# Pair products of a two-layer trunk: matmuls ordered by width, left operands prepared by parallel tasks, rotary tables begun earlier

## The chip, the cores and the metric

The kernel runs on one core of a Trainium2 chip, as one launch. The metric is the device time of one execution in microseconds; the time before is the median of three runs. All weights come from device memory in each execution.

## The reference

Two decoder layers over 512 positions, model width 1024, in float32. Each layer is a half-weighted gated feed-forward (FFN), a mixer (block-sparse attention in layer 0, a state-space mixer in layer 1), and another FFN. Cut to what the change touches, which are the four FFNs and the rotary tables of the attention:

```python
def swiglu(x, w_gate, w_up, w_down):
    return (jax.nn.silu(x @ w_gate) * (x @ w_up)) @ w_down

for i in range(2):
    x = x + 0.5 * swiglu(rms_norm(x, ffn1_norm[i]), ffn1_w_gate[i], ffn1_w_up[i], ffn1_w_down[i])
    h = rms_norm(x, mix_norm[i])
    x = x + moba_mixer(h, ...) if i == 0 else x + mamba2_mixer(h, ...)
    x = x + 0.5 * swiglu(rms_norm(x, ffn2_norm[i]), ffn2_w_gate[i], ffn2_w_up[i], ffn2_w_down[i])

# moba_mixer: q and k are turned by cos and sin of positions * inv_freq (rope)
```

The hidden width of an FFN is 2816, that is 22 tiles of 128.

## The kernel before

**Precision.** A float32 operand is split into a high part (rounded to the matmul's fp32r format) and a low part (the rest). A plain product then takes three matmuls: high by high, high by low, low by high. For weights, ScalarE (ACT) writes the high part (`whi`) from the loaded tile `wraw`, and VectorE (DVE) writes the low part (`wlo`). The task `halve_weights` does this piece by piece, 1024 columns at most, into a ring of four `whi` and four `wlo` buffers. Loads go out from SyncE's queue; a few sums of two weight tiles are made by accumulating transfers from GpSimd's (POOL's) queue.

**An FFN.** The hidden tiles stand in groups 0 to 5, 6 to 9, 10 to 13, 14 to 17 and 18 to 21 (`GROUPS`). Group 0 is computed plainly (`plain`). Each later group has two pairs of tiles (`pair`), and between their products stand the down projections of the group before (`down`). An FFN has eight pairs, so the four FFNs have 32 pairs.

**A pair.** For two hidden tiles, the 1024 inputs are cut in two halves and the 512 positions in two halves of 256, and a scheme of seven block products in place of eight is used. `PAIR` gives their order: A11, A12, A21-A22, -S2, A12-S2, a down projection, A11-A21, a down projection, A22, two down projections. The names are the left operands, blocks of the normed activations and their sums. Each left operand lies in four tiles `side` (k = 0 to 3) of 512 columns: 256 of the high part and 256 of the low part. One product (`product`) is, for two output halves o and four k, one matmul of 512 columns with `whi` (high weights by both parts) and one of 256 columns with `wlo` (low weights by the high part): 16 matmuls, alternating 512, 256, 512, 256. There are 32 x 7 = 224 products.

Products write three accumulators of two PSUM banks each: `x_`, `z_` and `y_`. Between products they are read: after A11 a task `read` copies half of `x_` (ACT) and adds the other half (DVE) into a tile; call it c1. After A12, `c11` makes two DVE additions from `z_`, and a gate follows (`ga`, ACT then DVE). After A21-A22 another `read` makes c5 from `y_`, again an ACT copy and a DVE addition. A12-S2 accumulates into `y_` and so may begin only when c5 has been read; the code waits for it with `yield When(lambda: "c5" in box)`. All those tiles are named `c` in the profile.

**Left operands.** The task `spread` (rank 60) makes the 28 `side` tiles of an FFN: for each k it scales two activation tiles into `xa` and `xb` (DVE), then one after the other, in place, the sums and differences (DVE, 256 columns), and for each left operand an ACT copy to the high part and a DVE subtraction for the low part (`sided`). One k is finished before the next begins.

**Order.** The order of instructions on every engine is written when the program is built, by a planner: tasks ask for tiles and instructions, and the planner issues the one that it thinks can start first, ties going to the lower rank. TensorE's main task has the rank `MAIN`; halving has `EASY` plus its due time, or `URGENT`. The chip then runs each engine's list in order, waiting on semaphores. The rotary tables (`rope_tables`: 14 small DVE operations, two sines on ACT, 18 POOL operations) are spawned by `midway`, at the first pair of group 3 of the first FFN, at rank `EASY - 1`, just ahead of the halving.

Most instructions are issued by one helper line (L221), so the profile is read by tile names.

Of the kernel before, what the change touches and what calls it, by code (L numbers as in the profile page):

```python
# [21 lines left out]
OP = mybir.AluOpType  # L22
# [18 lines left out]
GROUPS = ((0, 6), (6, 10), (10, 14), (14, 18), (18, 22))  # L41
# [10 lines left out]
MAIN, EASY, URGENT = 1e6, 1e5, -1.0  # L52
# [95 lines left out]
class Scheduler:  # L148
# [14 lines left out]
    def spawn(self, gen, prio=None):  # L163
        self.count += 1
        self.tasks.append(Task(gen, 100 + 0.01 * self.count if prio is None else prio))
        self.step(self.tasks[-1], None)
# [169 lines left out]
def trunk(ctx, tc, xT, pos, consts, cols, rows, wgu, wd, wqk, wv, wo, win, wz, wdt, wout, outT):  # L336
    nc = tc.nc
    V, S, PE, GP, SP = (Instructions(e, n) for e, n in (("DVE", nc.vector), ("ACT", nc.scalar), ("PE", nc.tensor), ("POOL", nc.gpsimd), ("SP", nc.sync)))
# [54 lines left out]
    def job(src, step=2.73, total=None, whole=False, term=None, name=None):  # L393


        n = src.shape[-1]
        if name:
            sources[name] = len(jobs)
        if term is not None:
            terms[len(jobs)] = sources[term] if isinstance(term, str) else term  # L400
        jobs.append((src, n, step, whole))
        needed.append(needed[-1] + (step * n / 512 if total is None else total))
# [24 lines left out]
    def down_job(i, what):  # L427
        job(down_src(i, what[2], what[1]))
# [5 lines left out]
    def pair_jobs(i, pair, downs):  # L434

        (b11, b21), (b12, b22) = ((wgu[i, j, :, :1024], wgu[i, j, :, 1024:]) for j in pair)
        right = {"A11": (b11, None), "A12": (b21, None), "A21-A22": (b12, b11), "-S2": (b22, "A21-A22"),
                 "A12-S2": (b22, None), "A11-A21": (b12, b22), "A22": (b21, "-S2")}
        downs = iter(downs)
        for nm in PAIR:  # L440
            if nm is None:
                down_job(i, next(downs))
            else:
                src, term = right[nm]
                job(src, step=2.78, total=2.78, whole=True, term=term, name=nm)

    for l in range(2):
        for i in (2 * l, 2 * l + 1):
# [140 lines left out]
    class Norm:  # L589
# [30 lines left out]
        def spread(self):  # L620


            yield When(lambda: self.rb is not None)
            for k in range(4):
                xa, xb = yield [slot("xa"), slot("xb")]
                for t, kk in ((xa, k), (xb, k + 4)):
                    op = V.scalar_tensor_tensor(t, x[kk], self.gain[:, kk:kk + 1], self.rb, op0=OP.mult, op1=OP.mult)
                    yield op.frees(*([self.rb] if kk == 7 and not self.plain else []))
                self.spread_left -= 2
                a11, a21, a12, a22 = xa[:, :256], xa[:, 256:], xb[:, :256], xb[:, 256:]  # L630
                yield from self.sided("A11", k, a11)
                yield from self.sided("A12", k, a12)
                yield from self.sided("A22", k, a22)
                yield V.tensor_tensor(a22, a21, a22, op=OP.subtract)
                yield from self.sided("A21-A22", k, a22)
                yield V.tensor_tensor(a22, a22, a11, op=OP.subtract)
                yield from self.sided("-S2", k, a22)
                yield V.tensor_tensor(a12, a12, a22, op=OP.add)
                yield from self.sided("A12-S2", k, a12, xb)
                yield V.tensor_tensor(a11, a11, a21, op=OP.subtract)  # L640
                yield from self.sided("A11-A21", k, a11, xa)

        def sided(self, nm, k, src, *done):
            t = yield slot("side", FR)
# [51 lines left out]
    def ffn(i, nrm, done, midway=None):  # L696
# [21 lines left out]
        def plain(j, last):  # L718
            p = take(wgu[i, j])
            pg, pu = yield [bank("pg"), bank("pu")]  # L720
            for u in range(2):
                for o, ps in ((0, pg), (1, pu)):
                    yield unit(p, 2 * u + o)
                    un = units[p][2 * u + o]
                    for kk in range(4):
                        k = 4 * u + kk
                        yield When(lambda: nrm.h[k] is not None)
                        ops = mm3(ps, cut(un, 128 * kk, 128 * kk + 128), nrm.h[k], k == 0, k == KT - 1)
                        if kk == 3:
                            ops[-1].frees(*un)  # L730
                        if last and o == 1:
                            ops[-1].frees(*nrm.h[k])
                        yield ops
            spawn(gated(pg, pu, j))

        def pair(j0, j1, downs, last):

# [2 lines left out]

            p = used[0]
            used[0] += 7 + len(downs)
            place = dict(zip(PAIR, range(p, p + len(PAIR))))
            out = {}

            def product(nm, ps, first):
                p = place[nm]
                Q.done_us = needed[p]
                yield unit(p, 0)
                un = units[p][0]  # L750
                for o in range(2):
                    for k in range(4):
                        yield When(lambda: nrm.left[nm][k] is not None)
                        a = nrm.left[nm][k]
                        b, c = 512 * o + 128 * k, 512 * o
                        ops = [PE.matmul(ps[:, c:c + 512], un[0][:, b:b + 128], a, start=first and k == 0, stop=False,
                                         skip_group_check=True),
                               PE.matmul(ps[:, c:c + 256], un[1][:, b:b + 128], a[:, :256], start=False, stop=k == 3,
                                         skip_group_check=True)]
                        if o and k == 3:  # L760
                            ops[-1].frees(*un)
                        if last and o:
                            ops[-1].frees(a)
                        yield ops

            def parts(ps):
                v = ps.rearrange("p (o h c) -> p o h c", o=2, h=2)
# [56 lines left out]
                yield from gate(j0, 1, t)  # L824

            x_, z_, y_ = None, None, None
            downs = iter(downs)
            seat = p
            for nm in PAIR:
                if nm is None:  # L830
                    assert used[0] > seat
                    keep, used[0] = used[0], seat
                    yield from down(*next(downs)[1:])
                    used[0] = keep
                elif nm == "A11":
                    x_ = yield bank("px", 2)
                    yield from product(nm, x_, True)
                    spawn(read(x_, "c1", box), 6)
                elif nm == "A12":
                    z_ = yield bank("pz", 2)  # L840
                    yield from product(nm, z_, True)
                    spawn(c11(z_), 6)
                elif nm == "A21-A22":
                    y_ = yield bank("py", 2)
                    yield from product(nm, y_, True)
                    spawn(read(y_, "c5", box), 6)
                elif nm == "-S2":
                    yield When(lambda: "c1" in box)
                    yield from product(nm, x_, False)
                    spawn(read(x_, "c2", box), 6)  # L850
                elif nm == "A12-S2":
                    yield When(lambda: "c5" in box)
                    yield from product(nm, y_, False)
                    spawn(c12(y_), 6)
                elif nm == "A11-A21":
                    yield When(lambda: "c2" in box)
                    yield from product(nm, x_, False)
                    spawn(c22(x_), 6)
                else:
                    yield When(lambda: "read" in box)  # L860
                    yield from product(nm, x_, False)
                    spawn(c21(x_), 6)
                seat += 1

        def down(g, n):
            p = take(down_src(i, n, g))
# [15 lines left out]
        for what in ffn_order(i):  # L882
            if isinstance(what, int):
                yield from plain(what, what == GROUPS[0][1] - 1)
            elif what[0] == "down":
                yield from down(*what[1:])
            else:
                if midway and what[0][0] == GROUPS[3][0]:
                    midway()
                yield from pair(*what[0], what[1], what[0] == (NH - 2, NH - 1))  # L890

# [477 lines left out]
    norms = [Norm(g) for g in gains]  # L1369

    def main():
        yield from ffn(0, norms[0], norms[1].add, lambda: spawn(rope_tables(), EASY - 1))
        yield from attention(norms[1], norms[2].add)
        yield from ffn(1, norms[2], norms[3].add)
        yield from ffn(2, norms[3], norms[4].add)
        yield from mamba(norms[4], norms[5].add)
        yield from ffn(3, norms[5], write)
# [94 lines left out]
```

## Time and profile before

| what | value |
|---|---|
| median of 3 runs | 2076.02 us (2075.43 to 2077.53) |
| profiled execution: its own time, its span | 2074.4 us, 2072.6 us |
| TensorE (PE) busy, share of the span | 2055.7 us, 99% |
| VectorE, ScalarE, GpSimd busy | 1490.8, 1034.4, 446.9 us |
| TensorE clock granted, mean of the span | 0.999 |
| matmul records: pair products, all | 3584, 10212 |

A busy PE is not a PE at its peak: matmuls overlap in the array, each record lasts longer than the distance to the next one, and the durations add up to more than the span. So the cost of a matmul is read as the distance from its start to the next start, and a wait shows as a distance that is longer than its neighbours'.

### The profile page before, as it was taken

How to read it: one execution, taken by the hardware profiler on the slowest of the kernel's cores; microseconds unless marked ns; L12 is line 12 of the kernel's file. 1: busy time of each engine (PE TensorE's matmuls, PEld its weight loads, DVE VectorE, ACT ScalarE, POOL GpSimd, SP SyncE). 2: the span in 40 equal slices, each digit the busy share in tenths (PEclk: the TensorE clock that was granted, in tenths of full speed). 3: DMA queues.
4: the chain of work that ended last, by engine and by line, in shares of the span. 5: the costliest groups of instructions: out<-in, count | busy, mean ns of one | idle time of the engine just before them, and what ended most of it. 6: DMA issues, size and time to landing. Idle time of an engine off the chain costs nothing.

```text
span 2072.6 us, 27874 instructions
## 1 busy us (share of the span) xinstructions
PE 2055.7 (99%) x10212; PEld 1721.8 (83%) x10212; DVE 1490.8 (72%) x2259; ACT 1034.4 (50%) x1756; POOL 446.9 (22%) x441
## 2 busy tenths in 40 slices
PE   9999999999999999999999999999999999999999
PEld 7788888888878888888888887888888888888887
DVE  6867877668879667778767776667575877767775
ACT  5544445454544444445444445674747645444442
POOL 1201211333231111102101011244343543101110
PEclk9999999999999999999999999999999999999999
DMA  7678895321135879854678884333332333678882
GB/s 251 159 190 213 207 229 154 102 67 66 62 107 129 203 200 225 216 164 117 179 190 213 219 212 150 91 94 112 91 103 92 102 112 110 153 194 210 218 217 77
DMA packets 102665, 321.31 MB, mean 155 GB/s; under 512 B 11520, under 2 KB 12160, under 8 KB 102528
## 3 DMA queue, kind: packets, MB, share of 16 engines
q1 hardware_dynamic: 84096, 252.42, 38.7%
q0 software_dynamic: 18432, 67.12, 18.5%
q8 instruction: 80, 1.31, 0.3%
q14 instruction: 57, 0.47, 0.1%
HBM read 283.77 MB, written 2.16 MB: 138 GB/s over the span
## 4 chain that ended last, share of the span: by engine, by line
PE 94%; DVE 3%; ACT 1%; POOL 1%; DMA 1%; issue 1%; SPq 0%; DVEq 0%; ACTq 0%; POOLq 0%
PE banks L221 94%; DVE wlo L221 1%; POOL ropea L221 0%; ACT whi L221 0%; DMA x<-xT 0%; DMA wraw<-wgu 0%; DVE c L221 0%; DVE xb L221 0%; DVE side L221 0%; SPq L221 0%; DVE xlo L221 0%; DVE ropeb L221 0%; POOL rstd L221 0%; ACT sq L221 0%; DVE rs_a L221 0%
## 5 line engine op out<-in xcount | busy, mean ns | idle before, releaser
L221 ACT ACTIVATE whi<-wraw 128x1024 fp32r<-128x1024 f32 (+1 forms) x531 | 498.2, 939 | 630.0 <-issue 303.2
L221 DVE TENSOR_TENSOR wlo<-wraw,whi 128x1024 fp32r<-128x1024 f32 (+1 forms) x531 | 589.2, 1111 | 188.0 <-ACT whi L221 187.3
L221 PE MATMUL banks<-side,whi 128*128 128x512 f32 x1792 | 639.3, 399 | 6.8 <-DVE c L221 4.0
L221 PE MATMUL banks<-side,wlo 128*128 128x256 f32 x1792 | 503.4, 281 | 0.7 <-DVE wlo L221 0.7
L221 PEld LDWEIGHTS banks<-side,whi 128*128 128x128 f32 x1792 | 336.7, 188 | 96.1 <-DVE c L221 14.5
L221 PEld LDWEIGHTS banks<-side,wlo 128*128 128x128 f32 x1792 | 338.7, 189 | 4.9 <-DVE wlo L221 1.2
L221 PE MATMUL banks<-hhi,whi 128*128 128x512 f32 x704 | 276.8, 393 | 0.0
L221 PE MATMUL banks<-hhi,wlo 128*128 128x512 f32 x704 | 275.5, 391 | 0.0
L221 PE MATMUL banks<-hlo,whi 128*128 128x512 f32 x704 | 274.7, 390 | 0.0
L221 PE MATMUL banks<-xhi,whi 128*128 128x512 f32 x648 | 259.1, 400 | 1.3 <-ACT xhi L221 1.3
L221 PE MATMUL banks<-xlo,whi 128*128 128x512 f32 x648 | 253.6, 391 | 1.4 <-DVE xlo L221 1.4
L221 PE MATMUL banks<-xhi,wlo 128*128 128x512 f32 x648 | 253.4, 391 | 0.0
L221 DVE TENSOR_TENSOR c<-banks,c 128x512 f32<-128x512 f32 x256 | 175.8, 687 | 45.3 <-PE banks L221 35.8
L221 PEld LDWEIGHTS banks<-hhi,wlo 128*128 128x128 f32 x704 | 132.2, 188 | 30.0
L221 PEld LDWEIGHTS banks<-hhi,whi 128*128 128x128 f32 x704 | 132.2, 188 | 28.8
L221 POOL DMA_DIRECT2D wraw<-wgu x64 | 56.5, 882 | 450.6 <-DMA wraw<-wgu 191.5
L221 DVE SCALAR_TENSOR_TENSOR x<-banks,x 128x512 f32<-128x512 f32 x160 | 110.4, 690 | 59.7 <-PE banks L221 58.6
L221 PEld LDWEIGHTS banks<-hlo,whi 128*128 128x128 f32 x704 | 132.4, 188 | 25.0
L221 POOL DMA_DIRECT2D wraw<-wraw x64 | 56.9, 888 | 441.8 <-DMA wraw<-wgu 210.7
L221 PEld LDWEIGHTS banks<-xlo,whi 128*128 128x128 f32 x648 | 121.6, 188 | 27.8 <-DVE xlo L221 2.6
L221 PEld LDWEIGHTS banks<-xhi,whi 128*128 128x128 f32 x648 | 121.5, 187 | 27.0 <-ACT xhi L221 1.6
L221 PEld LDWEIGHTS banks<-xhi,wlo 128*128 128x128 f32 x648 | 121.4, 187 | 26.4
(201 smaller groups left out, 2905.6 us busy)
## 6 DMA issues: line engine op xcount, KB each, us to landing
wraw<-wgu SPq DMA_DIRECT2D x270, 512.0 KB, 4.7
wraw<-wgu POOLq DMA_DIRECT2D x64, 512.0 KB, 8.2
wraw<-wraw POOLq DMA_DIRECT2D x64, 512.0 KB, 5.9
wraw<-wd SPq DMA_DIRECT2D x128, 256.0 KB, 4.1
wraw<-win SPq DMA_DIRECT2D x32, 512.0 KB, 3.8
wraw<-wd SPq DMA_DIRECT2D x32, 384.0 KB, 3.9
wraw<-wqk SPq DMA_DIRECT2D x16, 512.0 KB, 4.0
wraw<-wz SPq DMA_DIRECT2D x16, 512.0 KB, 3.8
```

Source lines behind the costliest of these rows:

```text
L221: op.fn(*op.args, **op.kw)
```

## The change

In `product` the two matmuls of a step are no longer issued together: all eight of 512 columns with `whi` come first, then all eight of 256 columns with `wlo`. In `spread` the one chain becomes four kinds of tasks with ranks of their own (60 to 66, by the order in which the products use the operands), with two more tiles per k (`xd`, `xe`) in place of sums made in place. `gated`, the gate of the plain tiles, gets rank 50. The rotary tables are spawned at the first pair of group 2 (hidden tiles 10 and 11) and not of group 3, two pairs sooner, at rank 2 x `EASY`, behind the halving. `pair_order` gives the order that `PAIR` gave, since every pair has four down projections.

```diff
+    def pair_order(downs):
+        rest = iter(downs)
+        order = [next(rest, None) if nm is None else nm for nm in PAIR]
+        return [nm for nm in order if nm is not None] + list(rest)
...
                 xa, xb = yield [slot("xa"), slot("xb")]
+                Q.uses[xa.tensor.name] = Q.uses[xb.tensor.name] = 4
...
-                a11, a21, a12, a22 = xa[:, :256], xa[:, 256:], xb[:, :256], xb[:, 256:]
-                yield from self.sided("A11", k, a11)
-                yield from self.sided("A12", k, a12)
-                yield from self.sided("A22", k, a22)
-                yield V.tensor_tensor(a22, a21, a22, op=OP.subtract)
-                yield from self.sided("A21-A22", k, a22)
-                yield V.tensor_tensor(a22, a22, a11, op=OP.subtract)
-                yield from self.sided("-S2", k, a22)
-                yield V.tensor_tensor(a12, a12, a22, op=OP.add)
-                yield from self.sided("A12-S2", k, a12, xb)
-                yield V.tensor_tensor(a11, a11, a21, op=OP.subtract)
-                yield from self.sided("A11-A21", k, a11, xa)
+                spawn(self.sided("A11", k, xa[:, :256], xa), 60)
+                spawn(self.sided("A12", k, xb[:, :256], xb), 61)
+                spawn(self.sided("A22", k, xb[:, 256:], xb), 66)
+                spawn(self.combined(k, xa, xb), 62)
+
+        def combined(self, k, xa, xb):
+            d = yield slot("xd")
+            Q.uses[d.tensor.name] = 4
+            yield V.tensor_tensor(d[:, :256], xa[:, 256:], xb[:, 256:], op=OP.subtract).frees(xa, xb)
+            spawn(self.sided("A21-A22", k, d[:, :256], d), 62)
+            yield V.tensor_tensor(d[:, 256:], d[:, :256], xa[:, :256], op=OP.subtract).frees(xa, d)
+            spawn(self.sided("-S2", k, d[:, 256:], d), 63)
+            e = yield slot("xe")
+            Q.uses[e.tensor.name] = 2
+            yield V.tensor_tensor(e[:, :256], xb[:, :256], d[:, 256:], op=OP.add).frees(xb, d)
+            spawn(self.sided("A12-S2", k, e[:, :256], e), 64)
+            yield V.tensor_tensor(e[:, 256:], xa[:, :256], xa[:, 256:], op=OP.subtract).frees(xa)
+            spawn(self.sided("A11-A21", k, e[:, 256:], e), 65)
...
-            spawn(gated(pg, pu, j))
+            spawn(gated(pg, pu, j), 50)
...
-                for o in range(2):
-                    for k in range(4):
-                        yield When(lambda: nrm.left[nm][k] is not None)
-                        a = nrm.left[nm][k]
-                        b, c = 512 * o + 128 * k, 512 * o
-                        ops = [PE.matmul(ps[:, c:c + 512], un[0][:, b:b + 128], a, start=first and k == 0, stop=False,
-                                         skip_group_check=True),
-                               PE.matmul(ps[:, c:c + 256], un[1][:, b:b + 128], a[:, :256], start=False, stop=k == 3,
-                                         skip_group_check=True)]
...
+                for h, w in ((0, 512), (1, 256)):
+                    for o in range(2):
+                        for k in range(4):
+                            yield When(lambda: nrm.left[nm][k] is not None)
+                            a = nrm.left[nm][k]
+                            b, c = 512 * o + 128 * k, 512 * o
+                            op = PE.matmul(ps[:, c:c + w], un[h][:, b:b + 128], a[:, :w], start=first and h == k == 0, stop=h == 1 and k == 3,
+                                           skip_group_check=True)
+                            if h and o and k == 3:
+                                op.frees(*un)
+                            if last and h and o:
+                                op.frees(a)
+                            yield op
...
-                if midway and what[0][0] == GROUPS[3][0]:
+                if midway and what[0][0] == GROUPS[2][0]:
...
-        yield from ffn(0, norms[0], norms[1].add, lambda: spawn(rope_tables(), EASY - 1))
+        yield from ffn(0, norms[0], norms[1].add, lambda: spawn(rope_tables(), 2 * EASY))
```

What the planner makes of it is seen in the engines' lists. On PE, at the first product of the first FFN (`xlo` and `xhi` are the normed activations of the plain tile ahead of it), before:

```order
L221 MATMUL banks<-xlo,whi 128x512
L221 MATMUL banks<-xhi,wlo 128x512
L221 MATMUL banks<-side,whi 128x512
L221 MATMUL banks<-side,wlo 128x256
L221 MATMUL banks<-side,whi 128x512
L221 MATMUL banks<-side,wlo 128x256
L221 MATMUL banks<-side,whi 128x512
```

and now:

```order
L221 MATMUL banks<-xlo,whi 128x512
L221 MATMUL banks<-xhi,wlo 128x512
L221 MATMUL banks<-side,whi 128x512 x8
L221 MATMUL banks<-side,wlo 128x256 x8
L221 MATMUL banks<-side,whi 128x512 x8
L221 MATMUL banks<-side,wlo 128x256 x8
```

All 224 products have the new form, and nothing else on PE has moved: the products, the down projections and the mixers follow each other as before.

On ACT, in a later pair of the second FFN (the first `c` copied is c1, the second c5, the third the next `read`; `ga` are gates), before:

```order
L221 ACTIVATE c_7606<-banks 128x512
L221 ACTIVATE whi<-wraw 128x512
L221 ACTIVATE ga<-c_7606 128x256
L221 ACTIVATE whi<-wraw 128x1024
L221 ACTIVATE c_7658<-banks 128x512
L221 ACTIVATE whi<-wraw 128x512
L221 ACTIVATE c_7686<-banks 128x512
L221 ACTIVATE whi<-wraw 128x1024
L221 ACTIVATE ga<-c_7686 128x256
L221 ACTIVATE whi<-wraw 128x512 x2
L221 ACTIVATE ga<-c_7658 128x256
```

and now:

```order
L221 ACTIVATE c_7623<-banks 128x512
L221 ACTIVATE whi<-wraw 128x512
L221 ACTIVATE ga<-c_7623 128x256
L221 ACTIVATE whi<-wraw 128x1024
L221 ACTIVATE c_7676<-banks 128x512
L221 ACTIVATE whi<-wraw 128x512
L221 ACTIVATE c_7702<-banks 128x512
L221 ACTIVATE whi<-wraw 128x1024
L221 ACTIVATE whi<-wraw 128x512
L221 ACTIVATE ga<-c_7702 128x256
L221 ACTIVATE whi<-wraw 128x512
L221 ACTIVATE ga<-c_7676 128x256
```

Up to the second `c` the list is the same; one gate has moved behind a `whi` of 512 columns. DVE's list between c1 and c5 is also unchanged in these pairs: two additions, a `wlo` of 512, an addition, a gate, a `wlo` of 1024, the addition of c5.

On DVE, at the first pair of the first FFN (`c_778` is c1 and then `c11`'s sum; `c_835` is c5), before:

```order
L221 TENSOR_TENSOR wlo<-wraw,whi 128x1024
L221 TENSOR_TENSOR c_778<-banks,c_778 128x512 x2
L221 TENSOR_TENSOR wlo<-wraw,whi 128x768
L221 TENSOR_TENSOR c_778<-banks,c_778 128x512
L221 TENSOR_TENSOR xa<-xa 128x256
L221 TENSOR_TENSOR hlo<-ga,hhi 128x512
L221 TENSOR_TENSOR ga<-banks,ga 128x512
L221 TENSOR_TENSOR wlo<-wraw,whi 128x1024
L221 TENSOR_TENSOR ga<-c_778,ga 128x256
L221 TENSOR_TENSOR c_835<-banks,c_835 128x512
```

and now (`c_796` and `c_848` take their place):

```order
L221 TENSOR_TENSOR wlo<-wraw,whi 128x1024
L221 TENSOR_TENSOR c_796<-banks,c_796 128x512
L221 TENSOR_TENSOR hlo<-ga,hhi 128x512
L221 TENSOR_TENSOR wlo<-wraw,whi 128x768
L221 TENSOR_TENSOR c_796<-banks,c_796 128x512 x2
L221 TENSOR_TENSOR ga<-banks,ga 128x512
L221 TENSOR_TENSOR c_848<-banks,c_848 128x512
L221 TENSOR_TENSOR ga<-c_796,ga 128x256
L221 TENSOR_TENSOR wlo<-wraw,whi 128x1024
```

The addition of c5 now stands ahead of a gate and a `wlo` of 1024, and the combination of `xa` is gone from here: all `side` tiles now stand ahead of c1.

## Rows read from the trace of the kernel before

**Rows 1.** The page: engines (busy us, share, instructions); the chain that ended last.
```profile
PE 2055.7 (99%) x10212; PEld 1721.8 (83%) x10212; DVE 1490.8 (72%) x2259; ACT 1034.4 (50%) x1756; POOL 446.9 (22%) x441
...
PE 94%; DVE 3%; ACT 1%; POOL 1%; DMA 1%; issue 1%; SPq 0%; DVEq 0%; ACTq 0%; POOLq 0%
```

**Rows 2.** The page's groups: count | busy us, mean ns of one | idle before, releaser.
```profile
L221 PE MATMUL banks<-side,whi 128*128 128x512 f32 x1792 | 639.3, 399 | 6.8 <-DVE c L221 4.0
L221 PE MATMUL banks<-side,wlo 128*128 128x256 f32 x1792 | 503.4, 281 | 0.7 <-DVE wlo L221 0.7
...
L221 PEld LDWEIGHTS banks<-side,wlo 128*128 128x128 f32 x1792 | 338.7, 189 | 4.9 <-DVE wlo L221 1.2
```

**Rows 3.** Timeline of PE, two products: start us, duration us.
```profile
861.98 0.40 PE L221 MATMUL banks<-side,whi 128*128 128x512 f32 x1
...
864.81 0.40 PE L221 MATMUL banks<-side,whi 128*128 128x512 f32 x1
...
873.54 0.39 PE L221 MATMUL banks<-side,whi 128*128 128x512 f32 x1
...
876.35 0.40 PE L221 MATMUL banks<-hhi,whi 128*128 128x512 f32 x1
```

**Rows 4.** Timeline of PE, an unbroken run of 512-column matmuls: first and 40th.
```profile
615.68 0.39 PE L221 MATMUL banks<-xhi,wlo 128*128 128x512 f32 x1
...
624.52 0.39 PE L221 MATMUL banks<-xhi,wlo 128*128 128x512 f32 x1
```

**Rows 5.** Timeline of PE, attention: three 256-column matmuls, twice; first and the next after.
```profile
426.71 0.29 PE L221 MATMUL banks<-pthi,vhi 128*128 128x256 f32 x1
...
427.08 0.22 PE L221 MATMUL banks<-pthi,vhi 128*128 128x128 f32 x1
...
492.90 0.28 PE L221 MATMUL banks<-pthi,vhi 128*128 128x256 f32 x1
...
493.25 0.22 PE L221 MATMUL banks<-pthi,vhi 128*128 128x128 f32 x1
```

**Rows 6.** Timeline of all engines, a later pair of the second FFN, around c5.
```profile
864.23 0.42 ACT L221 ACTIVATE ga<-c 128x256 f32<-128x256 f32 x1 [1.48 <-DVE c L221]
...
864.45 0.40 PE L221 MATMUL banks<-side,whi 128*128 128x512 f32 x1
...
864.69 0.28 PE L221 MATMUL banks<-side,wlo 128*128 128x256 f32 x1
...
864.93 1.06 ACT L221 ACTIVATE whi<-wraw 128x1024 fp32r<-128x1024 f32 x1 [0.29 <-PE banks L221]
...
866.03 1.23 DVE L221 TENSOR_TENSOR wlo<-wraw,whi 128x1024 fp32r<-128x1024 f32 x1 [0.92 <-ACT whi L221]
...
867.17 0.69 DVE L221 TENSOR_TENSOR c<-banks,c 128x512 f32<-128x512 f32 x1
...
867.51 0.28 PE L221 MATMUL banks<-side,wlo 128*128 128x256 f32 x1
...
867.91 0.49 PE L221 MATMUL banks<-side,whi 128*128 128x512 f32 x1
```

**Rows 7.** Who waited for tile `c`: waiter, us in all, times.
```profile
  PEld banks L221: 14.5, 26
```

**Rows 8.** Timeline of PE, first pair of the first FFN.
```profile
90.73 0.50 PE L221 MATMUL banks<-side,whi 128*128 128x512 f32 x1 [2.64 <-DVE c L221]
```

**Rows 9.** Groups of DVE by form: count | busy us, mean ns | idle before.
```profile
L221 DVE TENSOR_TENSOR wlo<-wraw,whi 128x1024 fp32r<-128x1024 f32 x366 | 467.6, 1279 | 159.3 <-ACT whi L221 158.8 <-DMA wraw<-win 0.2
...
L221 DVE TENSOR_TENSOR side<-xb,side 128x256 fp32r<-128x256 f32 x80 | 40.5, 518 | 8.0 <-ACT side L221 7.9
...
L221 DVE TENSOR_TENSOR xa<-xa 128x256 f32<-128x256 f32 x16 | 6.7, 418 | 0.0
```

**Rows 10.** Timelines of POOL, DVE and PE at the rotary tables, first FFN.
```profile
237.49 0.82 POOL L221 TENSOR_TENSOR ropecos<-cos,rowp 128x128 f32<-128x128 f32 x1
...
243.54 4.32 DVE L221 TENSOR_TENSOR wlo<-wraw,whi 128x1024 fp32r<-128x1024 f32 x2
...
246.59 0.39 PE L221 MATMUL banks<-side,wlo 128*128 128x256 f32 x1 [0.75 <-DVE wlo L221]
```

More of the change, by code (lines that the diff above doesn't have):

```diff
@@ L438, in pair_jobs @@
                  "A12-S2": (b22, None), "A11-A21": (b12, b22), "A22": (b21, "-S2")}
[L439 to L442, printed above, removed]
+        for nm in pair_order(downs):
+            if isinstance(nm, tuple):
+                down_job(i, nm)
             else:
@@ L742, in pair @@
             used[0] += 7 + len(downs)
-            place = dict(zip(PAIR, range(p, p + len(PAIR))))
+            order = pair_order(downs)
+            place = {nm: p + m for m, nm in enumerate(order)}
             out = {}
@@ L750, in product @@
                 un = units[p][0]
-                for o in range(2):
-                    for k in range(4):
-                        yield When(lambda: nrm.left[nm][k] is not None)
-                        a = nrm.left[nm][k]
-                        b, c = 512 * o + 128 * k, 512 * o
-                        ops = [PE.matmul(ps[:, c:c + 512], un[0][:, b:b + 128], a, start=first and k == 0, stop=False,
-                                         skip_group_check=True),
-                               PE.matmul(ps[:, c:c + 256], un[1][:, b:b + 128], a[:, :256], start=False, stop=k == 3,
-                                         skip_group_check=True)]
[L760 to L764, printed above, removed]
+                for h, w in ((0, 512), (1, 256)):
[11 more added lines that the diff above has]
+                            yield op
             def parts(ps):
@@ L826, in pair @@
             x_, z_, y_ = None, None, None
[L827 to L833, printed above, removed]
+            for nm in order:
+                if isinstance(nm, tuple):
+                    keep, used[0] = used[0], place[nm]
+                    yield from down(*nm[1:])
                     used[0] = keep
@@ L862, in pair @@
                     spawn(c21(x_), 6)
-                seat += 1
         def down(g, n):
```

## The prediction

> **What bounds the kernel.** I read the page's engine line and its chain first: TensorE is busy for 2055.7 us of 2072.6 and makes 94% of the chain that ended last [rows 1]. So a change counts by what it does to the distance between matmul starts, and by the few places where PE waits. Next I read the groups of the pair products: 1792 matmuls of 512 columns and as many of 256, with little idle time ahead of them, most of it ended by DVE's tile `c` [rows 2]. The means there (399 and 281 ns) are latencies of overlapping matmuls and no costs; the cost is a distance, so the third view is PE's timeline.
>
> A product of 16 matmuls takes 864.81 - 861.98 = 2.83 us when another product follows and 876.35 - 873.54 = 2.81 us when a down projection follows [rows 3]; I take 2.82. In an unbroken run of 512 columns, 39 distances take 8.84 us, 0.227 each [rows 4]. Runs of 256 columns exist only in the attention, three at a time: 0.37 us and 0.35 us, that is 0.123 and 0.117 each [rows 5].
>
> The fourth view is who waits for `c`: the weight loads do, 26 times [rows 7]. A typical case: the last narrow matmul of -S2 starts at 867.51, the first of A12-S2 not 0.12 later but 0.40 later, just after DVE's addition of c5 ends at 867.86 [rows 6]. 0.28 us is lost, 22 times in the 32 pairs by that same pattern; the other four are larger, the largest in the first pair of the first FFN, 2.64 us idle [rows 8]. Outside these, PE waits for a `wlo` once, while POOL makes rotary tables [rows 10].
>
> **The change part by part.**
>
> *Order by width.* After it a product is eight distances of 0.227 (1.816 us) and eight of a narrow run. With 0.120, the middle of the two runs, these are 0.960, in sum 2.776: 0.044 less than 2.82, times 224 products 9.9 us. Bounds: 0.117 gives 2.752 and 15.2 us; 0.123 gives 2.800 and 4.5 us. Further out, half of a wide distance (0.1135) gives 2.724 and 21.5 us; the break-even lies at (2.82 - 1.816) / 8 = 0.1255. I take 0.120, because the attention's run is the same kind of instruction, one 256-column operand after another into one bank, only shorter.
>
> [...]
>
> *The wait for c5.* A12-S2 waits for a chain: gate on ACT to 864.65, `whi` from 864.93 for 1.06 us, `wlo` from 866.03 for 1.23 us, c5 from 867.17 for 0.69 us, and PE starts 0.05 later [rows 6]. The `whi` waited for PE, for its buffer in the ring. It began at 864.93, before the last narrow matmul of that product was over (864.69 + 0.28 = 864.97) and after the last wide one was (864.45 + 0.40 = 864.85): what frees a `whi` buffer is the last matmul that reads it. With wide ones first, that one lies eight narrow distances, 0.96 us, before the product's end. Then the gate's end, 864.65, sets the start of `whi`; the rest of the chain keeps its order on ACT and DVE, moves 0.28 us forward, and lets PE start at 867.91 - 0.28 = 867.63. PE itself would be there at 867.51 + 0.12, less two products' gain of 0.044 each: 867.54. So about 0.08 of the 0.28 is left: 0.2 gained, 22 times, 4.4 us. Bounds: if the buffer is not free earlier, the two products' gain runs into a longer wait, -0.09 x 22 = -1.9 us; at most 0.28 x 22 = 6.2 us. What is late next is the gate's chain from A12, with nothing spare.
>
> *Parallel left operands.* The work is the same, 28 `side` tiles and 16 combinations in an FFN, and lies behind the plain tiles, 6 x 48 matmuls of 0.227 or 65 us. What moves is the order. In the first pair of the first FFN, one `side` and one combination more stand ahead of c1 (0.52 + 0.42 = 0.94 us), and between c1 and c5 a `wlo` of 1024 and two operations of 256 columns less (1.28 + 2 x 0.42 = 2.12 us) [rows 9]. So c5 comes 1.2 us sooner by DVE's queue; it can gain the full 2.64 idle [rows 8] if the waits of one k's chain between ACT and DVE also go. I take 2.0, bounds 1.2 and 2.6. The price is eight scalings in a row ahead of the second `wlo` of an FFN, some 7 us more queue; PE has four pieces in the ring, 4 x 24 matmuls x 0.227 = 22 us, and waited 0.7 us for `wlo` in all [rows 2], so I cost it at nothing. If that cover were gone, 7 us could be lost once in each FFN, 28 in all.
>
> *Rotary tables.* Eighteen POOL operations begin at 237.49, and two `wlo` of DVE, 1.28 us each by the mean, take 4.32 us then [rows 9, 10]; PE loses 0.75 idle [rows 10]. The Trainium skill, "SBUF — State Buffer", Who interferes with whom, says that a DVE operation with two SBUF inputs is blocked by a GpSimd operation that reads SBUF; the trace agrees (4.32 against 2.56). Moving the tables two pairs ahead moves this and does not remove it. DVE's small operations now stand among c1, c11 and c5 of their pair, behind the halving by rank. I take 0.5 gained, bounds 0.75 (that wait gone) and -1.5 (it comes three times). Rank 50 of the plain gates and `pair_order` cost nothing: the first reorders within the same 65 us, the second gives the old order.
>
> *Sum.* 9.9 + 4.4 + 2.0 + 0.5 = 16.8 us. The profiled execution took 2074.4 and would take 2057.6; the median of the runs lies 1.6 above it, so 2059.2, called 2059.
>
> **The rivals.**
>
> 1. *The order by width gives PE nothing*: the narrow run costs 0.1255, and only the waits shrink. For it: the first of the two attention runs has 0.123 [rows 5]. Against: the second has 0.117. PE is then no earlier at A12-S2 and the whole 0.28 goes, 6.2 us. The time: 2076.0 - 6.2 - 2.0 - 0.5 = 2067. Chance 0.15.
>
> 2. *The narrow run streams at half of a wide one*: PE would be at A12-S2 two times 0.096 sooner, so 0.09 of the wait goes and not 0.2, 2.0 us: 21.5 + 2.0 + 2.5 = 26.0, so 2050. For it: in 256 columns there is half of the work of 512. Against: neither attention run shows it. Chance 0.10.
>
> 3. *The weight load becomes the bound, slower*. Each matmul has a load of 128 columns whose record lasts 189 ns [rows 2]; in the old order every second load lies beside a 512-column matmul, in the new one eight follow each other beside 256 columns. If such a run settled at the load's 0.189, a product would take 1.816 + 1.512 = 3.33, 0.51 more, 224 times: 114 us slower, 2183 after the waits' gain. It decides from 0.1255 + 6.9 / (224 x 8) = 0.129 on; at 0.14, 26 us are lost and 2095 results. Against: three in a row in the attention come at 0.117 to 0.123 with loads of the same kind, so loads overlap each other. Chance 0.06. [...]
>
> 4. *Operands late*: the longer queues of `spread` or the tables eat 7 to 17 us and the time lies between 2066 and 2076. For it: the 7 us of longer queue in each FFN, with the tables' DVE and POOL work on top. Against: the ring's 22 us and the 0.7 us that PE waited for `wlo` in all [rows 2]. Chance 0.07.
>
> **How the numbers follow.** The forecast has 0.62, with 2053 to 2065 from 0.117 and 0.123 (5.3 either way) and the wait's bounds. To hold the time 8 times in 10 the range takes in rival 1 and half of rival 2: 2049 to 2069. Runs before spread over 2.1 us; 0.2%, or 4.2 us, is about what a measurement can tell here. Faster by more than that (below 2071.9): the forecast, rivals 1 and 2 and a third of rival 4, 0.89; I lower it to 0.87 for what I have not seen; within it 0.07; slower 0.06.
>
> **What would show it.** The 256-column run in PE's timeline: 0.120 from start to start, products of 2.78, and the busy time of PE less by about 10 us. The weight loads' wait for `c` in far fewer places or at under 0.1 us; ACT's `whi` starting right behind the gate. In the first FFN the 2.64 us gone or under 1. A wait for `wlo` of 0.5 to 2 us near the tables, some 60 us earlier. Wrong would be: narrow distances over 0.126; c5 waits of 0.28 or more in most pairs, which would mean that the ring's buffer is not freed sooner; waits for `side` or `wlo` in the plain tiles of any FFN.

## The result, and the profile after

The changed kernel takes 2051.3 us (median of four runs, 2049.8 to 2054.1) against 2076.0 us before: ratio 0.9881, 95% interval 0.9864 to 0.9898. It is 24.7 us faster where 16.8 were forecast, and inside the range of 2049 to 2069. The profiled execution took 2051.1 us, its span is 2049.3. The page of the kernel after: engines (PEld is TensorE's weight loads), then the chain that ended last:

```profile
PE 2039.5 (100%) x10212; PEld 1722.6 (84%) x10212; DVE 1483.6 (72%) x2259; ACT 1032.8 (50%) x1756; POOL 458.3 (22%) x441
...
PE 97%; DVE 1%; DMA 1%; POOL 0%; ACT 0%; issue 0%; SPq 0%; DVEq 0%
```

PE now makes 97% of the chain where it made 94% [rows 1]. The groups of the products after, as in [rows 2]:

```profile
L221 PE MATMUL banks<-side,whi 128*128 128x512 f32 x1792 | 447.0, 391 | 0.0
...
L221 PEld LDWEIGHTS banks<-side,wlo 128*128 128x128 f32 x1792 | 244.4, 190 | 17.5
...
L221 PE MATMUL banks<-side,wlo 128*128 128x256 f32 x1792 | 249.8, 282 | 0.0
```

By this view no idle time is left ahead of the products' matmuls. Their means have hardly moved (399 and 281 ns before), since they are latencies. The distances stand in PE's timeline, two products of the same pair of the second FFN as in [rows 6]; equal neighbours are one row, with their count behind the x; a row begins with start and duration in us:

```profile
843.62 1.98 PE L221 MATMUL banks<-side,whi 128*128 128x512 f32 x8
845.43 1.11 PE L221 MATMUL banks<-side,wlo 128*128 128x256 f32 x8
846.38 2.00 PE L221 MATMUL banks<-side,whi 128*128 128x512 f32 x8
848.23 1.11 PE L221 MATMUL banks<-side,wlo 128*128 128x256 f32 x8
849.18 0.63 PE L221 MATMUL banks<-side,whi 128*128 128x512 f32 x2
```

Eight narrow distances take 846.38 - 845.43 = 0.95 us, 0.119 each (0.120 was forecast). Eight wide ones take 1.81 us behind a down projection and 1.85 behind a product, so a product takes 2.76 or 2.80 us. All engines in that pair, from the gate to A12-S2:

```profile
851.30 0.42 ACT L221 ACTIVATE ga<-c 128x256 f32<-128x256 f32 x1 [2.20 <-DVE c L221]
851.63 1.04 ACT L221 ACTIVATE whi<-wraw 128x1024 fp32r<-128x1024 f32 x1
...
852.70 1.23 DVE L221 TENSOR_TENSOR wlo<-wraw,whi 128x1024 fp32r<-128x1024 f32 x1 [0.52 <-ACT whi L221]
...
853.85 0.68 DVE L221 TENSOR_TENSOR c<-banks,c 128x512 f32<-128x512 f32 x1
...
854.76 0.63 PE L221 MATMUL banks<-side,whi 128*128 128x512 f32 x2
```

The `whi` no longer waits for PE. It even starts 0.09 us before the gate's end (851.63 against 851.72). c5 ends at 854.53, and PE starts A12-S2 0.23 us later, as its own queue comes to it. In the view of who waited for `c`, no weight load is left among the waiters (26 before [rows 7]).

### The profile page after: what moved, and what is told of

Read it like the earlier page. It is cut to its first block, busy times and chain, and to the rows that moved or that the text cites. A ratio compares the mean times of both kernels' runs of the same rounds, so it can differ in the third digit from the quotient of the medians.

```text
span 2049.3 us, 27883 instructions
## 1 busy us (share of the span) xinstructions
PE 2039.5 (100%) x10212; PEld 1722.6 (84%) x10212; DVE 1483.6 (72%) x2259; ACT 1032.8 (50%) x1756; POOL 458.3 (22%) x441
## 4 chain that ended last, share of the span: by engine, by line
PE 97%; DVE 1%; DMA 1%; POOL 0%; ACT 0%; issue 0%; SPq 0%; DVEq 0%
PE banks L221 97%; DMA x<-xT 0%; DMA wraw<-wgu 0%; POOL ropea L221 0%; DVE acc L221 0%; SPq L221 0%; ACT whi L221 0%; DVE xlo L221 0%; POOL rstd L221 0%; DVE ropeb L221 0%; DVE ssq L221 0%; DVE rstd L221 0%; DVE ropea L221 0%; DVE x L221 0%; DVE wlo L221 0%
## 5 line engine op out<-in xcount | busy, mean ns | idle before, releaser
L221 PE MATMUL banks<-side,whi 128*128 128x512 f32 x1792 | 447.0, 391 | 0.0
L221 PEld LDWEIGHTS banks<-side,whi 128*128 128x128 f32 x1792 | 328.2, 188 | 63.9
L221 PEld LDWEIGHTS banks<-side,wlo 128*128 128x128 f32 x1792 | 244.4, 190 | 17.5
L221 PE MATMUL banks<-side,wlo 128*128 128x256 f32 x1792 | 249.8, 282 | 0.0
L221 ACT ACTIVATE ga<-c 128x256 f32<-128x256 f32 x128 | 53.1, 415 | 185.3 <-DVE c L221 185.3
```

The lines of the kernel that those rows point to most:

```text
L221: op.fn(*op.args, **op.kw)
```

## The experiments

Times are medians; ratios go to runs of the kernel before on the same chip, median 2075.6 to 2076.6 us.

**One part alone: the new product loop in the kernel before.** The edit is the third piece of the diff (`product`) and nothing else.

> The kernel before with the new product loop alone (eight wide, then eight narrow), left operands, gates and tables as before. Theory: the order by width saves 224 x 0.044 = 9.9 us and, since the whi buffer comes free 0.96 us sooner, the 22 waits of 0.28 us for c5 go whole, 6.2 us: 2076.0 - 16.1 = 2060 us, with c5 waits under 0.1 us, and the 2.6 us wait of the first pair of the first FFN and the tables' wait of about 0.9 us still there. Rival (the c5 waits went because the tasks were reordered): 2066 us with 22 waits of 0.28 us or more.

Measured: 2057.4 us, ratio 0.9908 (0.9895 to 0.9922). No c5 waits of 0.28 us. PE's timeline, the first pair and the tables of the first FFN:

```profile
91.30 0.47 PE L221 MATMUL banks<-side,whi 128*128 128x512 f32 x1 [2.03 <-DVE c L221]
...
243.91 0.50 PE L221 MATMUL banks<-hhi,wlo 128*128 128x512 f32 x1 [2.53 <-DVE wlo L221]
```

The loop brings 19 of the 25 us, where 16 were expected, and the rival falls. The first pair's wait stays, the tables' wait has grown from 0.75 us [rows 10] to 2.53, and PE waits twice for a gate (`ga`), 2.0 us in all, which was not expected.

**The rest alone: the changed kernel with the alternating product.**

> The changed kernel with the old alternating product; parallel left operands, gate rank and earlier tables stay. Theory: c5 waits of 0.28 us stay in about 22 pairs; the first pair of the first FFN loses 2.8 us of waiting, the tables about 1 us, and the start of the first FFN costs about 1.3 us more (waits for wlo and acc in its plain part): 2071 to 2073 us. Rival (the tasks remove the c5 waits): 2065 us and no wait of 0.28 us.

Measured: 2074.7 us, ratio 0.9992 (0.9983 to 1.0001): 1.9 us that can't be told from none. The view of who waited for `c` (us, times), and two starts of PE:

```profile
  PEld banks L221: 12.8, 25
```

```profile
88.87 0.49 PE L221 MATMUL banks<-side,whi 128*128 128x512 f32 x1 [2.02 <-DVE c L221]
...
172.55 0.50 PE L221 MATMUL banks<-hhi,wlo 128*128 128x512 f32 x1 [1.83 <-DVE wlo L221]
```

The c5 waits stay, as expected. Two things were not: the first pair still waits 2.02 us, so parallel operands alone don't remove [rows 8]'s 2.64; and tables that begin earlier still cost 1.83 us.

**One product of seven, added and taken away.** The new loop runs for A21-A22 alone, in the kernel before:

```diff
+                if nm == "A21-A22":
+                    for h, w in ((0, 512), (1, 256)):
...
+                else:
                     for o in range(2):
                         for k in range(4):
```

> The kernel before with one product of seven (A21-A22, the one whose whi buffer the late chain takes over) ordered by width, the other six alternating. Theory: 32 x 0.044 = 1.4 us of order and 22 x 0.28 = 6.2 us of waits, 2068.4 us, with the c5 waits under 0.1 us. Rival (the waits go because PE's order as a whole changes what ACT and DVE meet): 1.4 us or less, 2074.6 us, with 22 waits of 0.28 us.

Measured: 2065.5 us, ratio 0.9953 (0.9940 to 0.9965). None of the 22 waits of 0.28 us is left; the first pair still waits 1.94 us for c5, and the pair at the tables 0.51 us for a `c`. That is 11.1 us, against 7.6 expected and 1.4 by the rival: one product of seven takes the 22 waits away, because of its buffer. The reverse, with `if nm != "A21-A22":` in the changed kernel:

> The changed kernel with A21-A22 alone alternating again, the other six products by width. Theory: that buffer is freed at the product's end again, so a wait of 0.28 us, or of 0.37 with the 0.09 that PE is ahead, comes back in about 22 pairs: 6.2 to 8.1 us, and 1.4 us of order: 2051.3 + 7.6 to 9.5 = 2059 to 2061 us. Rival (order of tasks, or PE's order as a whole): 1.4 us alone, 2052.7 us.

Measured: 2065.0 us, ratio 0.9949 (0.9935 to 0.9963). All engines in that kernel, a later pair of the second FFN, and the view of who waited for `c`:

```profile
857.27 0.42 ACT L221 ACTIVATE ga<-c 128x256 f32<-128x256 f32 x1 [2.38 <-DVE c L221]
...
857.92 1.06 ACT L221 ACTIVATE whi<-wraw 128x1024 fp32r<-128x1024 f32 x1 [0.23 <-PE banks L221]
...
860.16 0.68 DVE L221 TENSOR_TENSOR c<-banks,c 128x512 f32<-128x512 f32 x1
...
860.90 1.45 PE L221 MATMUL banks<-side,whi 128*128 128x512 f32 x5 [0.17 <-DVE c L221]
```

```profile
  PEld banks L221: 12.7, 32
```

The `whi` waits for PE again, and all 32 pairs have the wait. The price, 13.7 us, is more than the 7.6 to 9.5 expected, because it hits 32 pairs and not 22, and because of what stands behind the wait (below).

**The buffer by itself.** The kernel before with the same list on every engine, and a fifth `whi` buffer in memory that the planner doesn't know of:

```diff
-            return Alloc(tag, lambda: pool.tile([p, n], dt, name=name, tag=tag, bufs=sizes[tag]))
+            return Alloc(tag, lambda: pool.tile([p, n], dt, name=name, tag=tag, bufs=5 if tag == "whi" else sizes[tag]))
```

> The kernel before, every engine's list the same, with five whi buffers in the chip's memory in place of four. Theory (A12-S2 waits because the late whi waits for its buffer): the 22 waits for c5 go, each 0.27 us ahead of A12-S2 and 0.07 us of slower start behind it: 7.5 us, 2076.6 - 7.5 = 2069 us, and 2067 us if the waits of 0.62 us for c in first pairs go too. Rival (the wait comes from the order of tasks on ACT and DVE, which is untouched here): 2076 us with 22 waits of 0.28 us.

Measured: 2067.6 us, ratio 0.9957 (0.9945 to 0.9970). All engines, the pair of [rows 6], from the gate to A12-S2:

```profile
861.67 0.42 ACT L221 ACTIVATE ga<-c 128x256 f32<-128x256 f32 x1 [3.64 <-DVE c L221]
...
862.00 1.04 ACT L221 ACTIVATE whi<-wraw 128x1024 fp32r<-128x1024 f32 x1
...
864.22 0.68 DVE L221 TENSOR_TENSOR c<-banks,c 128x512 f32<-128x512 f32 x1
...
865.20 0.40 PE L221 MATMUL banks<-side,whi 128*128 128x512 f32 x1
```

With no order changed the wait is gone, and c5 is 0.30 us early (864.22 + 0.68 against 865.20). None of the 22 pairs has it any more; the first pair of the first FFN still waits, 2.34 us. Together with the two runs before it, this settles the cause of the 22 waits: A12-S2 waited since a `whi` far down its chain waited for A21-A22 to let go of its buffer.

**What a pair costs.** The start of A11 in two pairs that follow each other gives the length of a whole pair. PE's timelines, one fence each: five buffers, the changed kernel, and the changed kernel with A21-A22 alternating:

```profile
853.91 0.39 PE L221 MATMUL banks<-side,whi 128*128 128x512 f32 x1
...
884.68 0.39 PE L221 MATMUL banks<-side,whi 128*128 128x512 f32 x1
```

```profile
874.05 0.39 PE L221 MATMUL banks<-side,whi 128*128 128x512 f32 x1
```

```profile
849.40 0.39 PE L221 MATMUL banks<-side,whi 128*128 128x512 f32 x1
...
880.30 0.39 PE L221 MATMUL banks<-side,whi 128*128 128x512 f32 x1
```

Alternating without a wait is 30.77 us, by width 874.05 - 843.62 = 30.43 (the first start stands in the fence of the two products; the loop alone has 30.43 too). So the order by width alone is worth 0.34 a pair, 32 x 0.34 = 10.9 us. One product put back costs 30.90 - 30.43 = 0.47 in a pair, 15.0 us in all by this sum. That is more than the 13.7 measured: seven pairs, which have a small wait in the changed kernel already (below), pay only about 0.26.

**Half of the order.** The two outer loops of the new `product` change places: 4 wide, 4 narrow, 4 wide, 4 narrow.

> The changed kernel with the order by width inside each output half: 4 wide, 4 narrow, 4 wide, 4 narrow. Theory: each step from narrow to wide costs 0.027 us in the distances of the wide ones behind it (2.793 against 2.766 us for a product), and there are 224 more of them: 6.0 us, 2057 us; whi is freed 0.48 us before the product's end, more than the 0.28 that was missing, so no c5 waits. Rival A (only strict alternation costs something): 2051 us. Rival B (0.48 us is not enough): c5 waits of 0.1 us or more in most pairs, 3 us or more on top, 2060 us and over.

Measured: 2057.7 us, ratio 0.9914 (0.9900 to 0.9928). PE's timeline, A22 between two down projections:

```profile
2016.00 1.07 PE L221 MATMUL banks<-side,whi 128*128 128x512 f32 x4
2016.91 0.64 PE L221 MATMUL banks<-side,wlo 128*128 128x256 f32 x4
2017.38 1.09 PE L221 MATMUL banks<-side,whi 128*128 128x512 f32 x4
2018.31 0.63 PE L221 MATMUL banks<-side,wlo 128*128 128x256 f32 x4
```

The first four wide take 0.91 us, the four behind narrow ones 0.93, and the product 2.78 against 2.76. A pair (A11 at 847.03, the next at 877.63) takes 30.60 us, 0.17 more than in the changed kernel, 5.3 us in all. So rival A falls. The theory's time came out, but not all by its steps: a product is 0.014 us longer where 0.027 was expected, the down projections behind products are 0.02 longer, and A12-S2's first distance is 0.28 us where 0.235 is usual behind a product; c5 is ready only 0.11 us ahead of it there, against 0.23 in the changed kernel. Rival B's waits of 0.1 us and over are not there in the later pairs; the first pair of the first FFN has one of 0.28.

**The other parts, each taken back alone.** The tables at their old place and rank:

> The changed kernel with the rotary tables at their old place and rank. Theory (POOL and DVE get in each other's way wherever the tables run in one block): a wait for wlo of 0.9 to 2.7 us comes back near 240 us of the span: 2051.3 + 0.9 to 2.7 = 2052.2 to 2054 us. Rival (the order by width has already made room for the tables): 2051.3 us and no such wait.

Measured: 2054.7 us, ratio 0.9896 (0.9883 to 0.9910). DVE's and PE's timelines at the tables:

```profile
236.69 5.43 DVE L221 TENSOR_TENSOR wlo<-wraw,whi 128x512 fp32r<-128x512 f32 x4
```

```profile
238.57 0.50 PE L221 MATMUL banks<-hhi,wlo 128*128 128x512 f32 x1 [2.07 <-DVE wlo L221]
```

The wait is back, 2.07 us. The four `wlo` of that row are one of 512 columns and three of 1024: the first takes 1.83 us, where 0.69 is usual, the second 1.40, and the last two, behind the tables' end at 239.21, the usual 1.2. The old chain of left operands with the old rank of the gates:

> The changed kernel with the old chain of left operands and the old rank of the plain gates; order by width and early tables stay. Theory: the waits of 0.83, 1.44 and 2.19 us of the first FFN that the kernel with the new product loop alone showed come back, 4.5 us, and the 1.3 us at the start of the first FFN (waits for wlo and acc) go: 2051.3 + 3.2 = 2054.5 us, 2053 to 2057. Rival (the order by width alone is enough): 2050 us, no wait over 0.5 us in the first pair.

Measured: 2054.6 us, ratio 0.9899 (0.9885 to 0.9912). The first pair waits 2.03 us for c5 again, as the kernel with the loop alone does. The intervals of these two runs overlap the changed kernel's (0.9864 to 0.9898), so what each part is worth is read from the waits and not from the medians. The old rank of the gates alone, `spawn(gated(pg, pu, j))`:

> The changed kernel with the old rank of the plain gates; parallel left operands stay. Theory (the wait of 2.2 us for c5 in the first pair is gone since all side tiles stand ahead of c1, so that c5 can stand ahead of a wlo of 1024 columns): no such wait, the changed kernel's time within 1 us. Rival (the gates' rank did it): 2.2 us for c5 and 0.5 to 1.5 us for a gate in the first pair, the changed kernel's time and 3 us.

Measured: 2055.5 us, ratio 0.9900 (0.9885 to 0.9915). PE's timeline in the plain part of the first FFN, and the windows around it (us, PE busy and matmuls, granted clock, DMA share and GB/s):

```profile
57.87 0.47 PE L221 MATMUL banks<-xhi,whi 128*128 128x512 f32 x1 [3.38 <-DVE ga L221]
...
59.38 0.63 PE L221 MATMUL banks<-xhi,wlo 128*128 128x512 f32 x1
59.80 0.63 PE L221 MATMUL banks<-xhi,whi 128*128 128x512 f32 x1
```

```profile
58.90:62.30 3.40, 3.40 (x10) 0.52 0.83 156
...
62.40:67.00 4.60, 4.60 (x22) 1.00 0.52 185
```

The theory is half right. A12-S2 doesn't wait for c5 in the first pair, so with the new loop it is the parallel operands that moved it. But without rank 50 the plain gate stands behind a row of `side` tiles on DVE, the last eleven of them from 52.79 to 57.04 us; PE waits 3.38 us for it, and some 1 us later runs 3.4 us at a granted clock of 0.52, matmuls 0.42 to 0.43 us apart.

**Towards a better kernel.** The changed kernel once more:

> The changed kernel once more, beside the three others. Theory (the waits of 0.70 us for wlo and 1.32 us for acc in its first 26 us come from a load that landed late in that execution, since the same lists showed 0.64 us and no wlo wait in the kernel with late tables): other sizes there now, acc near 0.65 us; every pair without a c5 wait; 2051 to 2054 us. Rival (they belong to the new order of tasks): 0.70 and 1.32 us again.

Measured: 2050.5 us, ratio 0.9877 (0.9862 to 0.9892). PE waits 0.44 us for `acc` where the first execution waited 1.16, and not for `wlo` at the start, where that one waited 0.53: those go with the execution, since the lists are the same. But the first pair has a c5 wait now, which the theory excluded. PE's timeline there:

```profile
87.90 0.50 PE L221 MATMUL banks<-side,whi 128*128 128x512 f32 x1 [0.32 <-DVE c L221]
```

Narrow eight first in the four products that accumulate:

> The changed kernel with the narrow eight first in the four products that accumulate (-S2, A12-S2, A11-A21, A22); the three that open an accumulator stay wide first. Their whi then comes free at the product's end, that of A21-A22 as early as in the changed kernel. Theory (A21-A22's buffer is the one that counts, and a step from narrow to wide costs 0.027 us, six in a pair in place of seven): no c5 wait of 0.28 us, 0.9 us less at most: 2050.4 to 2052 us. Rival (the other buffers count too): waits of 0.1 us or more in most pairs, 3 us or more on top.

Measured: 2055.1 us, ratio 0.9902 (0.9886 to 0.9919). Later pairs are 0.01 to 0.03 us shorter, some 0.5 us in all, where the theory allowed 0.9, without c5 waits of 0.28. But the planner made other lists, and near the tables PE waits 1.28 us for `wlo` and 2.33 for `c`. Neither the theory nor the rival had that.

The changed kernel with a fifth `whi` buffer:

> The changed kernel, every list the same, with five whi buffers in the chip's memory. Theory (after the change PE no longer waits for anything behind a whi buffer): no change beyond 1 us. Rival (the ring still holds something back): 2 us or more faster, with the sum of waits in the first FFN smaller.

Measured: 2050.4 us, ratio 0.9877 (0.9862 to 0.9891): no change against the 2050.5 beside it. No kernel here beats the changed one by more than the runs can tell.

## Why the prediction was right, and where its sum was not

The two profiled executions differ by 2074.4 - 2051.1 = 23.3 us. By the lengths of the pairs this is: order by width 10.9; c5 waits 6.5; the first pair of the first FFN 3.2; the pair at the tables 2.0, half of it the tables' (their 0.75 idle [rows 10] and a slower start behind it) and half two waits for `c`; two more waits for `c` of about 0.6, with what stands behind them, 1.4. Against it, the first pair begins 0.55 later (76.89 us for 76.34). That makes some 23.4. Of the four others of [rows 7], which the prediction calls larger than 0.28, three are; the one at the tables is 0.23.

**Order by width, 9.9 forecast, 10.9 measured.** The mechanism and the distance were right: 0.119 for 0.120. A product is 0.03 to 0.05 shorter, as forecast (0.044). The rest comes behind it: the down projections after A11-A21 and A22 take 2.75 and 5.47 us in the changed kernel, 2.78 and 5.50 behind the alternating products of the kernel with five buffers. Rivals 1 to 3 are out, and rival 4 too: the one wait for `wlo` in a plain part, 0.53 us, was not there when the kernel ran again. Pairs without any wait are 0.34 us shorter, the narrow distance is neither 0.1135 nor at the load's 0.190. The Trainium skill, "TensorE: Matmul & The Clock Gate", Back-to-back issue gap, gives N/2.4 + 2.5 ns for the gap of an isolated matmul, by which both orders would cost the same, and says that in a stream of loads and matmuls both set the spacing. The rows go against the first for this stream: the same instructions cost 30.77 or 30.43 us a pair by their order alone. Whether the loads are the reason is not shown.

**The wait for c5, 4.4 forecast, 6.5 measured: the term that was mis-sized.** The cause was right and is shown by three runs, one of which adds nothing but the buffer. The step that failed is "about 0.08 of the 0.28 is left". Measured, c5 ends 0.23 us ahead of A12-S2, and for three reasons the sum ran short. First, it set `whi` to the gate's end, but ACT starts it 0.09 us sooner once nothing holds it. Second, it looked at one buffer. A `whi` earlier in the pair began only as A11 ended, 2.94 us after A11's start, and begins at 2.06 now; it delayed c1, c1 stood ahead of c11 on DVE, and so the gate was late too. From the start of A21-A22, the gate ended after 864.65 - 861.98 = 2.67 us [rows 3, 6] and now after 851.72 - 849.18 = 2.54. Third, a wait costs more than its length: behind one, the first two matmuls stand further apart. By the length of a pair, 887.44 - 856.34 = 31.10 us in the kernel before (its next A11 starts at 887.44) against 30.77 without the wait, a c5 wait cost 0.33 and not 0.28. Other pairs are up to 31.19 long, and the 22 together lost 8.0 us, so that even the upper bound, 6.2, was too low. In return, seven pairs, the first two of the FFNs as a rule, have a new small wait that makes them about 0.2 longer, and an eighth pair one of 0.06, 1.5 us in all. PE's timeline of one:

```profile
122.95 1.11 PE L221 MATMUL banks<-side,wlo 128*128 128x256 f32 x8
123.99 0.73 PE L221 MATMUL banks<-side,whi 128*128 128x512 f32 x2
```

The eight narrow take 1.04 us instead of 0.95, and the two wide 0.73 instead of the 0.63 at 854.76.

**Parallel left operands, 2.0 forecast, 3.2 measured in the first pair, but not by these tasks alone.** Some 2.9 of it is the wait for c5, and 0.3 one for a gate. With the tasks alone the first pair waits 2.02 us for c5, with the loop alone 2.03, with both not at all, or 0.32 when the kernel ran again. There PE came to this pair 0.84 us sooner and the pair was 0.81 longer, so the start and the first pair together brought 2.6 to 2.7 us in both executions. DVE's timeline in the changed kernel, first pair, shows why:

```profile
85.01 0.68 DVE L221 TENSOR_TENSOR ga<-banks,ga 128x512 f32<-128x512 f32 x1
86.11 0.69 DVE L221 TENSOR_TENSOR c<-banks,c 128x512 f32<-128x512 f32 x1 [0.42 <-ACT c L221]
86.72 0.41 DVE L221 TENSOR_TENSOR ga<-c,ga 128x256 f32<-128x256 f32 x1
87.05 1.22 DVE L221 TENSOR_TENSOR wlo<-wraw,whi 128x1024 fp32r<-128x1024 f32 x1
```

c5 stands ahead of the `wlo` of 1024 columns here; with the tasks alone, and with the loop alone, that `wlo` is ahead of it. That rank 50 of the plain gates costs nothing was right for the whole change and hid its worth: without it the tasks cost a wait of 3.38 us and the half clock behind it. So the price was not the queue ahead of a `wlo` but the gate behind the side tiles, and the rank pays it.

**Tables, 0.5 forecast, 1.0 measured.** The sum was near, but the step was wrong: the wait went instead of moving. In the changed kernel the 18 POOL operations are spread over 19 us, in a group of 5 and one of 13. The `wlo` beside them are still held up, but less: two of 512 columns take 1.23 and 0.98 us and one of 1024 1.43, where late tables stretch one of 512 to 1.83. PE waits for none of them. An early start by itself isn't what does it: with the alternating product the early tables still cost 1.83 us. POOL's timeline in the changed kernel, the first and the last of the 18:

```profile
159.08 0.81 POOL L221 TENSOR_TENSOR ropecos<-cos,rowp 128x128 f32<-128x128 f32 x1
...
177.18 1.24 POOL L221 TENSOR_SCALAR ropesin<-ropesin 128x256 f32<-128x256 f32 x1
```

**Open.** The median with late tables lies 3.4 to 4.2 us above the changed kernel's, and rows show 2.1 us idle; its profiled execution was its fastest, 2051.6 us. What made the others longer was not seen in a trace; they have a granted clock of 0.999 and the fastest 1.000, so a stretch at half clock as below may be part of it. Nor was it tried why the planner puts c5 or the tables where it does in each list.

## What to carry to other kernels

When a matmul waits for a chain, walk the chain back to its first wait: here it was a ring buffer, held by matmuls that a change of order within one product could finish sooner. An extra buffer that the order doesn't know of tests this in one run, with every list the same. Group matmuls of one width, and where a planner writes the lists, price a change by whole runs and not part by part: the loop alone gave 19 us, the rest alone 2, both 25.

## What the runs showed of the hardware

- A wait has a tail: the first distance behind it is about 0.1 us longer (two wide matmuls end after 0.73 us and not 0.63).
- A step from narrow to wide matmuls costs 0.02 to 0.04 us in the wide ones behind it (eight take 1.85 us and not 1.81, four 0.93 and not 0.91), and steady alternation is dearer than two runs (30.77 us a pair and not 30.43).
- Behind a wait the granted clock can fall to about 0.5, the lower of its two levels, 1.2 GHz, and need not. It fell some 1 us behind the end of waits of 3.38 us (old rank of the gates), 2.34 us (five buffers, first pair) and 2.03 us (old operands); behind 2.64 us in the kernel before and 2.03 us with the loop alone it stayed at 1.00. The windows for the five buffers:

```profile
92.50:95.80 3.30, 3.30 (x12) 0.50 0.95 231
```

- The same is seen at the start of the first FFN. In the kernel before, behind waits of 1.28 and 0.29 us, the windows show a granted clock of 0.52 for 2.9 us, and the full clock behind it:

```profile
8.40:11.30 2.90, 2.90 (x8) 0.52 1.05 380
11.30:14.00 2.70, 2.70 (x13) 1.00 1.08 295
```

Eight matmuls stand 0.43 us apart there, some 1.5 us lost. The changed kernel's profiled execution has full clock in its first 15 us, its run with five buffers again 0.50. The lists there are the same in these two, so this goes with the execution, and may be part of the spread of 2 us and more between runs.
